# An encoder layer on one core: the last w_up stores on GpSimd's queue, and w_down's weights, late loads and weight sums placed behind left tiles

## The chip, the cores and the metric

The kernel runs on 1 core of one Trainium2 chip. The metric is the device time of one execution in microseconds (us). A core has five engines with a queue of instructions each, taken in program order: TensorE (PE, matmuls; PEld its weight loads), VectorE (DVE), ScalarE (ACT), GpSimd (POOL) and SyncE (SP). Transfers between DRAM and SBUF are issued by an engine, here nearly all by SP, and carried out by 16 DMA engines. Engines wait for each other by semaphores.

## The reference

One layer of an encoder on 2048 tokens of width 1024: two kinds of attention, gates, an output product, and then a feed-forward block. Only that block and the last norm concern this change:

```python
h2 = rms_norm(x, norm_mlp[l])
x = x + jnp.square(jax.nn.relu(h2 @ w_up[l])) @ w_down[l]
return rms_norm(x, norm_final)
```

`w_up` is 1024 x 4096 and `w_down` 4096 x 1024, everything in float32.

## The kernel before

**Products.** A float32 product is made of three matmuls (`mm3s`, L285 to L288): each operand is split into a high part, rounded by ACT (L282), and a low part, the rest, by DVE (L283); high x high is L286, high x low L287, low x high L288. On top of that, a matrix product is cut into 2 x 2 blocks and made of seven block products instead of eight, numbered 1 to 7, whose operands are blocks or sums of blocks, and whose results are added into the four output blocks.

**w_up.** For each half of the tokens (`m` = 0, 1) eight steps `q` go over the columns of w_up (`up_quad`). Each makes the seven products, and from their results, after ReLU (L1527, L1529) and square (L1530), the left tiles of w_down's seven products: blocks `uc`, sums `uchunk` and `urb`. They go to DRAM arrays `at`: `keep` (L1550) stores those of w_down's products 3 to 7. Products 1 and 2 of w_down are cut a second time into seven (`TWICE = (1, 2)`); their left tiles go to `at2[n][p]` through `keep2` (L1575). Those of p = 1, 2, 4 are the blocks themselves; for p = 5, 6, 7, 3, with m = 1, two stored blocks are read back into a tile `urb` (L1561, on POOL's queue) and added to the new ones on DVE. All stores are issued by SP, all in one order with its loads.

**w_down.** Product order is 1, 6, 2, 7, 5, 3, 4. The ordinary ones (6, 7, 5, 3, 4) take 16 steps `k`: a left tile `da` (512 KB, L1856, four buffers), its split `dah` (four buffers), a right tile (256 KB of weights `dw`, L1863, eight buffers, or a sum of such), its split `dwh` (four buffers), and 24 matmuls of 512 columns into eight PSUM banks. Product 6 also makes `t2[k]` (L1868): two differences of three `dw` blocks, kept for products 7, 5 and 4. Products 1 and 2 go through `twice` (L1900): seven sub-products in the order 1, 5, 6, 2, 7, 3, 4 of four steps each, 24 matmuls of 256 columns a step; a left tile `da` at L1924, the right tile a block, or a sum of blocks, of four weight tiles `ZW0` to `ZW3`, which `twice_right` loads (L1882, 16 loads of 256 KB). For product 2 the sums are made ahead (`twice_sums`, called in step 7 of product 6). `add_x2` (L1966) loads a piece of the residual and adds it to an output block; the adds are spread over the steps of later products (`later`). `gf`, the last norm's weights, is loaded and scaled by POOL (L2034, L2035) behind product 1.

**The order.** The code names the engine of each instruction. The position of an instruction in its engine's queue comes from a scheduler that goes by a modelled timeline and takes an instruction when its operands and buffers are expected to be ready; so a load for a later product can stand ahead of a load for an earlier one. `tc.issue_after(x)` makes what is in its block stand behind `x` in that order. The rings of w_down take the memory that w_up's rings leave, so the first instructions on them wait for w_up's last uses.

Of the kernel before, what the change touches and what calls it, by code (L numbers as in the profile page):

```python
# [92 lines left out]
def encoder_layer(ctx, tc, x, norm_mix, w_in, b_gate, sink, rpb, w_pa, w_pb, w_out,  # L93
# [52 lines left out]
    def bcast(ap1d, n):  # L146
        return bass.AP(ap1d.tensor, ap1d.offset, [[0, P], [1, n]])
# [1392 lines left out]
    def up_quad(m, q, lf, right, spread, each, rest=()):  # L1540
# [6 lines left out]

        def keep(n, a, c):
            if n not in TWICE:
                stored[0] = SY.dma_start(ats[n][2 * q + a][:, m], c).ins  # L1550
                return
            if (m, a) != (1, 0):
                keep2(n, {(0, 0): 1, (0, 1): 2, (1, 1): 4}[m, a], c)
            if m == 0:
                return
            if a == 0:
                first[n] = c
                return
            t = up_rings["rb"]()
            for i in range(2):  # L1560
                G.dma_start(t[:, i], at2[n][1 + i][q // 2][:, q % 2])  # L1561
            a11, a12, s1, s2 = (t[:, i] for i in range(4))
            add(V, s1, first[n], c)
            keep2(n, 5, s1)
            add(V, s2, s1, a11, ALU.subtract)
            keep2(n, 6, s2)
            add(V, a11, a11, first[n], ALU.subtract)
            keep2(n, 7, a11)
            add(V, a12, a12, s2, ALU.subtract)
            keep2(n, 3, a12)  # L1570
# [1 line left out]
        first = {}  # L1572

        def keep2(n, p, c):
            stored[0] = SY.dma_start(at2[n][p][q // 2][:, q % 2], c).ins  # L1575

        for n in (1, 5, 6, 2, 7, 4, 3):
            hl, (rh, rl) = lf[n], right[n]
# [274 lines left out]
    def left(n, k, part=None):  # L1853
        raw, hl = da(), dah()
        use = slice(0, 2) if part is None else slice(part, part + 1)
        SY.dma_start(raw[:, use], ats[n][k][:, use])  # L1856
        split(raw[:, use], hl[:, 0, use], hl[:, 1, use], V)
        return hl

    def w_block(k, p, j):  # L1860
        f = 4 * (k // 2) + 2 * p + k % 2
        w = dw()
        SY.dma_start(w, w_down[0][f * P : (f + 1) * P, j * BT : (j + 1) * BT])  # L1863
        return w

    t2 = [None] * 16
# [1 line left out]
    def make_t2(k):  # L1868
        b11, b12, b22 = w_block(k, 0, 0), w_block(k, 0, 1), w_block(k, 1, 1)
        t2[k] = t2_()  # L1870
        add(V, b12, b22, b12, ALU.subtract)
        add(V, t2[k], b12, b11)

    def twice_right(n):

        p, j = {1: (0, 0), 2: (1, 0)}[n]
        out = [zw() for zw in zws]
        for a in range(2):
            for qq in range(4):
                for i in range(2):  # L1880
                    f = 4 * (2 * qq + i) + 2 * p + a
                    SY.dma_start(out[qq][:, 2 * i + a], w_down[0][f * P : (f + 1) * P, j * BT : (j + 1) * BT])  # L1882
        return [r.rearrange("p (i a) (j c) -> p i a j c", a=2, j=2) for r in out]

    def wide(t):
        return t.rearrange("p (i c) -> p i c", i=2)

    def twice_sums(rs):

        out = []  # L1890
        for r in rs:
            b11, b12, b22 = r[:, :, 0, 0], r[:, :, 0, 1], r[:, :, 1, 1]
            t1, t2 = wide(p5_()), wide(p5_())
            add(V, t1, b12, b11, ALU.subtract)
            add(V, t2, b22, t1, ALU.subtract)
            add(V, b12, b22, b12, ALU.subtract)
            out.append((t1, t2))
        return out

    def twice(n, rs, sums=None):  # L1900

        b = [bank() for _ in range(4)]
        n_bank[0] += 2
        x, z, y = b[:2], b[2:], [bank() for _ in range(2)]

        def right(p, k):

            b11, b12, b21, b22 = (rs[k][:, :, a, j] for a in range(2) for j in range(2))
            t1, t2 = sums[k] if sums else (b11, b11)
            src = {1: b11, 2: b21, 3: b22, 5: t1, 6: t2, 7: b12, 4: t2}[p]  # L1910
            if p == 4:
                add(V, src, b21, t2, ALU.subtract)
            elif not sums and p in (5, 6, 7):
                add(V, src, *{5: (b12, b11), 6: (b22, b11), 7: (b22, b12)}[p], ALU.subtract)
            hl = dwh()
            hi, lo = (wide(hl[:, i]) for i in range(2))
            split(src, hi, lo, V)
            return hi, lo

        for p in ORDER_3:  # L1920
            acc = {1: x, 2: x, 5: z, 3: z, 6: y, 7: y, 4: y}[p]
            for k in range(4):
                raw, lf = da(), dah()
                SY.dma_start(raw, at2[n][p][k])  # L1924
                split(raw, lf[:, 0], lf[:, 1], V)
                hi, lo = right(p, k)
                for t in range(4):
                    ps = acc[t // 2][:, t % 2 * 256 : t % 2 * 256 + 256]
                    at = slice(t * P, (t + 1) * P)
                    for i in range(2):  # L1930
                        mm3s(ps, lf[:, 0, i, at], lf[:, 1, i, at], hi[:, i], lo[:, i],
                             p in (1, 5) and t % 2 == 0 and k == 0 and i == 0, k == 3 and i == 1)
            for i in range(2):
                ps = wide(acc[i])
                top, low = ((X2[2 * h + i][:, :, 0:256], X2[2 * h + i][:, :, 256:512]) for h in range(2))
                if p == 1:
                    A.copy(y[i], x[i])
                    continue
                out = {5: low[1], 6: top[1], 2: top[0], 7: low[1], 3: top[1], 4: low[0]}[p]
                if n == 1 and p in (5, 6, 2, 4):  # L1940
                    A.copy(out, ps)
                else:
                    add(V, out, ps, out)
# [19 lines left out]
    def add_x2(c, i, j, t):  # L1963
        r = row_of(i, t)
        xt = x2_()
        SY.dma_start(xt, x2d[r // BT][r % BT : r % BT + P, j * BT : (j + 1) * BT])  # L1966
        add(V, c, c, xt)

    sums = {}
# [54 lines left out]
            squares(Z[t], 1, 0, t)  # L2024
            finish((Z[t], W[t]), 1, t)

    ready = {1: [twice_right(1)]}
    for n in (1, 6, 2, 7, 5, 3, 4):
        if n in TWICE:
            twice(n, *ready[n])  # L2030
            if n == 2:
                later.extend((lambda t=t: early(X[t], 0, t)) for t in range(8))
            else:
                SY.dma_start(gf, bcast(norm_final, D))  # L2034
                G.tensor_scalar(gf, gf, float(D) ** 0.5, 1.0, ALU.mult, ALU.mult)  # L2035
            continue
        if n == 6 and 2 in TWICE:
            ready[2] = [twice_right(2)]
        if n == 7:
            for rows, tiles in ((Z, zws[:2]), (W, zws[2:])):  # L2040
                rows.extend(r[:, i] for zw in tiles for r in (zw(),) for i in range(4))
        for group in ((range(8),) if n != 4 else (range(4), range(4, 8))):
# [9 lines left out]
            for k in range(16):  # L2052
                if n == 6:
                    make_t2(k)
                    if k == 7 and 2 in TWICE:
                        ready[2].append(twice_sums(ready[2][0]))
                lf, rt = left(n, k, part), right_(n, k)

                if k >= end:
# [46 lines left out]
```

## Time and profile before

| what | value |
|---|---|
| median of 3 runs | 2589.79 us (2588.19 to 2592.97) |
| the profiled execution, own time | 2584.19 us |
| its span in the trace | 2582.3 us (1.9 us lie around it) |
| mean granted PE clock | 0.995 |
| ACT busy | 1353.9 us (52%) |
| DMA | 590.25 MB, mean 229 GB/s |
| last w_up matmul ends | 1957.99 us |
| product 1 of w_down starts, ends | 1964.22, 2057.41 us |

The page gives busy times by engine; the trace behind it can be asked for any stretch. Below, "PE's waits" lists what ended PE's idle times; a timeline row has start, duration, engine, line, operation, output and inputs, and in brackets the idle time before it with its releaser; "the chain of waits" is followed back from the last instruction; SPq is SP issuing a transfer, and DMA share is the mean busy share of the 16 DMA engines.

### The profile page before, as it was taken

The page shows a single profiled execution, that of the slowest core. Times are in us where ns is not written, and L with a number is a line of the kernel's source. Part 1 is how long each engine was busy: PE and PEld are TensorE (multiplying, and loading weights), DVE is VectorE, ACT ScalarE, POOL GpSimd, SP SyncE. Part 2 cuts the span into 40 slices and gives each one's busy share as a digit, 9 for nine tenths or more (in the row PEclk, how much of TensorE's full clock was granted, in tenths as well). Part 3 has the DMA queues.
Part 4 walks back from the last instruction along what each step waited for, and adds up shares of the span by engine and source line. Part 5 has one row for each costly group of instructions (what it writes and reads, how often), then busy time and mean ns, then how long its engine had stood idle before and what let it go on. Part 6 is the DMA issues. An engine that isn't in the chain of part 4 may idle for free.

```text
span 2582.3 us, 36197 instructions
## 1 busy us (share of the span) xinstructions
PE 2529.6 (98%) x12512; PEld 2137.7 (83%) x12512; DVE 1779.9 (69%) x2786; ACT 1353.9 (52%) x2421; POOL 421.8 (16%) x533
## 2 busy tenths in 40 slices
PE   8999999999999999999999999999997999999998
PEld 6788888878888888888888878888887989988887
DVE  8857676656665677656587776887777947754766
ACT  6365464557776676424255665644444534422444
POOL 1000101133446765120310000000000000000011
PEclk9999999999999999999999999999998999999999
DMA  5768868774357999688886877876659944644564
GB/s 188 222 196 255 281 216 273 245 219 122 106 148 194 242 278 258 217 305 310 300 315 208 264 257 254 300 236 218 213 198 334 370 168 157 214 158 157 184 201 162
DMA packets 365159, 590.25 MB, mean 229 GB/s; under 512 B 33912, under 2 KB 158312, under 8 KB 362928
## 3 DMA queue, kind: packets, MB, share of 16 engines
q1 hardware_dynamic: 345232, 539.03, 65.4%
q0 software_dynamic: 8800, 24.79, 3.1%
q10 hardware_dynamic: 10944, 24.12, 2.5%
q8 instruction: 99, 1.62, 0.3%
q14 instruction: 84, 0.69, 0.1%
HBM read 388.52 MB, written 199.30 MB: 228 GB/s over the span
## 4 chain that ended last, share of the span: by engine, by line
PE 83%; DMA 7%; DVE 5%; ACT 2%; issue 1%; SPq 1%; POOL 0%; DVEq 0%; POOLq 0%; ACTq 0%
PE b L288 16%; PE b L286 16%; PE b L287 16%; PE zb L286 5%; PE zb L288 5%; PE zb L287 5%; PE mm L202 3%; PE mm L204 3%; PE mm L203 3%; PE av L1141 2%; PE pt L1161 2%; PE s L1115 2%; PE pt L897 1%; DMA h2d<-ht 1%; PE av L883 1%
## 5 line engine op out<-in xcount | busy, mean ns | idle before, releaser
L286 PE MATMUL b<-dwh,dah 128*128 128x512 f32 (+1 forms) x1088 | 367.9, 347 | 11.7 <-ACT dah L282 11.7
L287 PE MATMUL b<-dwh,dah 128*128 128x512 f32 (+1 forms) x1088 | 376.3, 347 | 0.0
L288 PE MATMUL b<-dwh,dah 128*128 128x512 f32 (+1 forms) x1088 | 368.8, 347 | 2.1 <-DVE dah L283 2.1
L282 ACT CAST dah<-da 128x1024 fp32r<-128x1024 f32 (+1 forms) x152 | 145.5, 960 | 273.9 <-PE b L288 141.8
L286 PE MATMUL zb<-zh,zwhl 128*128 128x512 f32 x728 | 284.8, 392 | 3.2 <-ACT zc L493 1.4
L283 DVE TENSOR_TENSOR dah<-da,dah 128x1024 fp32r<-128x1024 f32 (+1 forms) x152 | 168.4, 1110 | 169.7 <-ACT dah L282 169.5
L287 PE MATMUL zb<-zh,zwhl 128*128 128x512 f32 x728 | 285.1, 392 | 0.0
L288 PE MATMUL zb<-zh,zwhl 128*128 128x512 f32 x728 | 283.4, 391 | 0.8 <-DVE zwhl L283 0.8
L286 PEld LDWEIGHTS b<-dwh,dah 128*128 128x128 f32 x1088 | 207.9, 191 | 37.6 <-ACT dah L282 12.8
L286 PE MATMUL b<-ubh,uwhlb 128*128 128x512 f32 x592 | 230.2, 389 | 1.2 <-DVE uc L277 1.2
L287 PE MATMUL b<-ubh,uwhlb 128*128 128x512 f32 x592 | 230.3, 389 | 0.0
L288 PE MATMUL b<-ubh,uwhlb 128*128 128x512 f32 x592 | 229.1, 389 | 0.3 <-DVE uwhlb L283 0.3
L288 PEld LDWEIGHTS b<-dwh,dah 128*128 128x128 f32 x1088 | 206.0, 191 | 28.0 <-DVE dah L283 2.8
L287 PEld LDWEIGHTS b<-dwh,dah 128*128 128x128 f32 x1088 | 207.8, 191 | 24.9
L286 PEld LDWEIGHTS zb<-zh,zwhl 128*128 128x128 f32 x728 | 136.9, 188 | 33.4 <-ACT zc L493 2.5
L288 PEld LDWEIGHTS zb<-zh,zwhl 128*128 128x128 f32 x728 | 136.9, 188 | 29.3 <-DVE zwhl L283 1.3
L287 PEld LDWEIGHTS zb<-zh,zwhl 128*128 128x128 f32 x728 | 137.0, 188 | 27.8
L202 PE MATMUL mm<-zh,whl 128*128 128x512 f32 x368 | 156.0, 424 | 2.3 <-DVE z L1019 1.2
L204 PE MATMUL mm<-zh,whl 128*128 128x512 f32 x368 | 145.8, 396 | 0.0
L203 PE MATMUL mm<-zh,whl 128*128 128x512 f32 x368 | 145.5, 395 | 0.0
L277 DVE TENSOR_TENSOR uc<-b,uc 128x512 f32<-128x512 f32 x160 | 108.4, 685 | 48.7 <-PE b L288 46.7
L286 PEld LDWEIGHTS b<-ubh,uwhlb 128*128 128x128 f32 x592 | 111.1, 188 | 24.6 <-ACT uchunk L1347 1.6
(276 smaller groups left out, 5826.4 us busy)
## 6 DMA issues: line engine op xcount, KB each, us to landing
da<-at SPq DMA_DIRECT2D x120, 512.0 KB, 4.2
at<-uc SPq DMA_DIRECT2D x172, 256.0 KB, 3.7
uraw<-in_w_up_dram SPq DMA_DIRECT2D x32, 1024.0 KB, 6.0
dw<-in_w_down_dram SPq DMA_DIRECT2D x128, 256.0 KB, 3.9
pgl<-wo_d SPq DMA_DIRECT2D x28, 1024.0 KB, 6.3
zraw<-in_w_in_dram SPq DMA_DIRECT2D x24, 1024.0 KB
z<-zg SPq DMA_DIRECT2D x64, 256.0 KB, 5.3
at<-urb SPq DMA_DIRECT2D x64, 256.0 KB, 2.2
```

What stands on the lines that cost most here:

```text
L202: PE.matmul(ps, lh, rh, start=first, stop=False)
L203: PE.matmul(ps, lh, rl, start=False, stop=False)
L204: PE.matmul(ps, ll, rh, start=False, stop=last)
L277: return eng.tensor_tensor(out=out, in0=a, in1=b, op=op).ins
L282: rounded[0] = A.copy(hi, src).ins
L283: return eng.tensor_tensor(out=lo, in0=src, in1=hi.bitcast(F32), op=ALU.subtract).ins
L286: PE.matmul(ps, lh, rh, start=first, stop=False, skip_group_check=True)
L287: PE.matmul(ps, lh, rl, start=False, stop=False, skip_group_check=True)
L288: PE.matmul(ps, ll, rh, start=False, stop=last, skip_group_check=True)
L1115: PE.matmul(ps[:, :n], q[:, i, :], kv[:, z, B_R0[i] // 4 : (B_R0[i] + B_NR[i]) // 4, 4 * B_C0[j] : 4 * (B_C0[j] + w)], start=z == 0, stop= ...
L1141: PE.matmul(po[0][:, i0 * P : (i0 + ni) * P], v[:kp, c, :], src[:kp, o : o + ni * P], start=first[0], stop=(c == 7 and z == 1), skip_group ...
L1161: last = PE.transpose(pt[:kp, at + (i - i0) * P : at + (i - i0 + 1) * P], s[i][:, rr : rr + kp], ident)
```

## The change

- Of the stores of the second token half, those of p = 5, 6, 7, 3 for products 1 and 2, and in the last step (q = 7) all, are issued by POOL instead of SP: 76 stores.
- `twice_right` no longer issues its 16 loads at once. It returns a generator that issues two at a time: for product 1 one pair ahead of each left tile, for product 2 one pair in each step of product 6 from step 2 on.
- Each `dw` load stands behind the load of the third last left tile, each `x2` load and `gf` behind the last one; the first difference of `t2` and of each set of sums stands behind the last left tile's low part on DVE.
- The four sets of sums for product 2 are made one at a time in steps 8, 10, 12 and 14 of product 6.
- `gf` is loaded ahead of product 7 and scaled by ACT.

```diff
--- before.py
+++ after.py
@@ -1547,7 +1547,8 @@
 
         def keep(n, a, c):
             if n not in TWICE:
-                stored[0] = SY.dma_start(ats[n][2 * q + a][:, m], c).ins
+                queue = G if m and q == 7 else SY
+                stored[0] = queue.dma_start(ats[n][2 * q + a][:, m], c).ins
                 return
             if (m, a) != (1, 0):
                 keep2(n, {(0, 0): 1, (0, 1): 2, (1, 1): 4}[m, a], c)
@@ -1572,7 +1573,8 @@
         first = {}
 
         def keep2(n, p, c):
-            stored[0] = SY.dma_start(at2[n][p][q // 2][:, q % 2], c).ins
+            queue = G if m and (q == 7 or p in (5, 6, 7, 3)) else SY
+            stored[0] = queue.dma_start(at2[n][p][q // 2][:, q % 2], c).ins
 
         for n in (1, 5, 6, 2, 7, 4, 3):
             hl, (rh, rl) = lf[n], right[n]
@@ -1853,14 +1855,17 @@
     def left(n, k, part=None):
         raw, hl = da(), dah()
         use = slice(0, 2) if part is None else slice(part, part + 1)
-        SY.dma_start(raw[:, use], ats[n][k][:, use])
-        split(raw[:, use], hl[:, 0, use], hl[:, 1, use], V)
+        das.append(SY.dma_start(raw[:, use], ats[n][k][:, use]).ins)
+        last_lo[0] = split(raw[:, use], hl[:, 0, use], hl[:, 1, use], V)
         return hl
+
+    last_lo, das = [None], []
 
     def w_block(k, p, j):
         f = 4 * (k // 2) + 2 * p + k % 2
         w = dw()
-        SY.dma_start(w, w_down[0][f * P : (f + 1) * P, j * BT : (j + 1) * BT])
+        with tc.issue_after(das[-3]):
+            SY.dma_start(w, w_down[0][f * P : (f + 1) * P, j * BT : (j + 1) * BT])
         return w
 
     t2 = [None] * 16
@@ -1868,36 +1873,40 @@
     def make_t2(k):
         b11, b12, b22 = w_block(k, 0, 0), w_block(k, 0, 1), w_block(k, 1, 1)
         t2[k] = t2_()
-        add(V, b12, b22, b12, ALU.subtract)
+        with tc.issue_after(last_lo[0]):
+            add(V, b12, b22, b12, ALU.subtract)
         add(V, t2[k], b12, b11)
 
     def twice_right(n):
 
         p, j = {1: (0, 0), 2: (1, 0)}[n]
         out = [zw() for zw in zws]
-        for a in range(2):
-            for qq in range(4):
-                for i in range(2):
-                    f = 4 * (2 * qq + i) + 2 * p + a
-                    SY.dma_start(out[qq][:, 2 * i + a], w_down[0][f * P : (f + 1) * P, j * BT : (j + 1) * BT])
-        return [r.rearrange("p (i a) (j c) -> p i a j c", a=2, j=2) for r in out]
+
+        def load():
+            for a in range(2):
+                for qq in range(4):
+                    for i in range(2):
+                        f = 4 * (2 * qq + i) + 2 * p + a
+                        SY.dma_start(out[qq][:, 2 * i + a], w_down[0][f * P : (f + 1) * P, j * BT : (j + 1) * BT])
+                    yield
+
+        return [r.rearrange("p (i a) (j c) -> p i a j c", a=2, j=2) for r in out], load()
 
     def wide(t):
         return t.rearrange("p (i c) -> p i c", i=2)
 
     def twice_sums(rs):
 
-        out = []
         for r in rs:
             b11, b12, b22 = r[:, :, 0, 0], r[:, :, 0, 1], r[:, :, 1, 1]
             t1, t2 = wide(p5_()), wide(p5_())
-            add(V, t1, b12, b11, ALU.subtract)
+            with tc.issue_after(last_lo[0]):
+                add(V, t1, b12, b11, ALU.subtract)
             add(V, t2, b22, t1, ALU.subtract)
             add(V, b12, b22, b12, ALU.subtract)
-            out.append((t1, t2))
-        return out
-
-    def twice(n, rs, sums=None):
+            yield t1, t2
+
+    def twice(n, rs, loads, sums=None):
 
         b = [bank() for _ in range(4)]
         n_bank[0] += 2
@@ -1920,9 +1929,10 @@
         for p in ORDER_3:
             acc = {1: x, 2: x, 5: z, 3: z, 6: y, 7: y, 4: y}[p]
             for k in range(4):
+                next(loads, None)
                 raw, lf = da(), dah()
-                SY.dma_start(raw, at2[n][p][k])
-                split(raw, lf[:, 0], lf[:, 1], V)
+                das.append(SY.dma_start(raw, at2[n][p][k]).ins)
+                last_lo[0] = split(raw, lf[:, 0], lf[:, 1], V)
                 hi, lo = right(p, k)
                 for t in range(4):
                     ps = acc[t // 2][:, t % 2 * 256 : t % 2 * 256 + 256]
@@ -1963,7 +1973,8 @@
     def add_x2(c, i, j, t):
         r = row_of(i, t)
         xt = x2_()
-        SY.dma_start(xt, x2d[r // BT][r % BT : r % BT + P, j * BT : (j + 1) * BT])
+        with tc.issue_after(das[-1]):
+            SY.dma_start(xt, x2d[r // BT][r % BT : r % BT + P, j * BT : (j + 1) * BT])
         add(V, c, c, xt)
 
     sums = {}
@@ -2024,19 +2035,19 @@
             squares(Z[t], 1, 0, t)
             finish((Z[t], W[t]), 1, t)
 
-    ready = {1: [twice_right(1)]}
+    ready = {1: list(twice_right(1))}
     for n in (1, 6, 2, 7, 5, 3, 4):
         if n in TWICE:
             twice(n, *ready[n])
             if n == 2:
                 later.extend((lambda t=t: early(X[t], 0, t)) for t in range(8))
-            else:
-                SY.dma_start(gf, bcast(norm_final, D))
-                G.tensor_scalar(gf, gf, float(D) ** 0.5, 1.0, ALU.mult, ALU.mult)
             continue
         if n == 6 and 2 in TWICE:
-            ready[2] = [twice_right(2)]
+            ready[2] = list(twice_right(2))
         if n == 7:
+            with tc.issue_after(das[-1]):
+                SY.dma_start(gf, bcast(norm_final, D))
+            A.activation(gf, gf, AF.Copy, scale=float(D) ** 0.5)
             for rows, tiles in ((Z, zws[:2]), (W, zws[2:])):
                 rows.extend(r[:, i] for zw in tiles for r in (zw(),) for i in range(4))
         for group in ((range(8),) if n != 4 else (range(4), range(4, 8))):
@@ -2052,8 +2063,13 @@
             for k in range(16):
                 if n == 6:
                     make_t2(k)
-                    if k == 7 and 2 in TWICE:
-                        ready[2].append(twice_sums(ready[2][0]))
+                    if k >= 2 and 2 in TWICE:
+                        next(ready[2][1], None)
+                    if k == 6 and 2 in TWICE:
+                        sums2 = twice_sums(ready[2][0])
+                        ready[2].append([])
+                    if k >= 8 and k % 2 == 0 and 2 in TWICE:
+                        ready[2][2].append(next(sums2))
                 lf, rt = left(n, k, part), right_(n, k)
 
                 if k >= end:
```

How the rows move where w_up gives way to w_down, first on **SP**. Before, the tail of the `ZW` loads and the first left tiles (`da`, sub-product 1, `at1_1_k`):

```order
L1882 DMA ZW2_2024_18319<-in_w_down_dram 128x512 x2
L1882 DMA ZW0_2022_18317<-in_w_down_dram 128x512 x2
L1550 DMA at4_15_11490<-uc_2003_18141 128x512
L1882 DMA ZW1_2023_18318<-in_w_down_dram 128x512 x2
L1882 DMA ZW2_2024_18319<-in_w_down_dram 128x512 x2
L1924 DMA da_2026_18343<-at1_1_0_11539 128x1024
L1924 DMA da_2029_18375<-at1_1_1_11540 128x1024
L1924 DMA da_2032_18407<-at1_1_2_11541 128x1024
L1924 DMA da_2035_18439<-at1_1_3_11542 128x1024
L1863 DMA dw_2114_19299<-in_w_down_dram 128x512
L1550 DMA at5_14_11505<-uchunk_2006_18205 128x512
L1863 DMA dw_2115_19301<-in_w_down_dram 128x512
```

and further on, where the first left tile of sub-product 5 (`at1_5_0`) stands:

```order
L1966 DMA x2_2355_21140<-x2d0_148 128x512
L1575 DMA at2_6_3_11578<-urb_2004_18178 128x512
L1966 DMA x2_2361_21179<-x2d2_150 128x512
L1924 DMA da_2038_18473<-at1_5_0_11543 128x1024
L1966 DMA x2_2367_21218<-x2d2_150 128x512
L1966 DMA x2_2373_21257<-x2d2_150 128x512
L1550 DMA at5_15_11506<-uchunk_2008_18230 128x512
L1575 DMA at2_7_3_11586<-urb_2004_18178 128x512
L1575 DMA at2_3_3_11590<-urb_2004_18178 128x512
L1966 DMA x2_2379_21296<-x2d2_150 128x512
L1924 DMA da_2041_18506<-at1_5_1_11544 128x1024
```

Now, from the first `ZW` load on:

```order
L1890 DMA ZW3_2025_18320<-in_w_down_dram 128x512 x4
L1890 DMA ZW0_2022_18317<-in_w_down_dram 128x512 x2
L1934 DMA da_2026_18329<-at1_1_0_11539 128x1024
L1890 DMA ZW1_2023_18318<-in_w_down_dram 128x512 x2
L1934 DMA da_2029_18363<-at1_1_1_11540 128x1024
L1890 DMA ZW2_2024_18319<-in_w_down_dram 128x512 x2
L1934 DMA da_2032_18397<-at1_1_2_11541 128x1024
L1934 DMA da_2035_18431<-at1_1_3_11542 128x1024
L1890 DMA ZW0_2022_18317<-in_w_down_dram 128x512 x2
L1890 DMA ZW1_2023_18318<-in_w_down_dram 128x512 x2
L1890 DMA ZW2_2024_18319<-in_w_down_dram 128x512 x2
L1934 DMA da_2038_18467<-at1_5_0_11543 128x1024
```

The left tiles stand between the pairs of `ZW`; the stores are gone from here, and `dw`, `x2` and `gf` no longer stand ahead of sub-product 5.

On **DVE**, around the low part of the first left tile (`dah_2027`), before:

```order
L277 TENSOR_TENSOR ZW1_2023_18318<-ZW1_2023_18318 128x2x256
L277 TENSOR_TENSOR uc_2005_18204<-uc_1995_17996,uchunk_2006_18205 128x512
L277 TENSOR_TENSOR ZW3_2025_18320<-ZW3_2025_18320 128x2x256
L277 TENSOR_TENSOR ZW2_2024_18319<-ZW2_2024_18319 128x2x256
L277 TENSOR_TENSOR urb_2004_18178<-urb_2004_18178 128x512
L283 TENSOR_TENSOR dah_2027_18344<-da_2026_18343,dah_2027_18344 128x1024
L277 TENSOR_TENSOR ZW3_2025_18320<-ZW3_2025_18320 128x2x256
L277 TENSOR_TENSOR uchunk_2008_18230<-uc_1998_18067,uc_2003_18141 128x512
L277 TENSOR_TENSOR urb_2004_18178<-urb_2004_18178,uc_1995_17996 128x512
```

and now, where `dwh_2028` is the low part of the first right tile:

```order
L277 TENSOR_TENSOR urb_2001_18100<-urb_2001_18100 128x512
L277 TENSOR_TENSOR uc_2003_18141<-b_152_18054,uc_1996_18011 128x512
L283 TENSOR_TENSOR dwh_2028_18334<-ZW0_2022_18317,dwh_2028_18334 128x512
L277 TENSOR_TENSOR uc_2003_18141<-b_150_18026,uc_2003_18141 128x512
L277 TENSOR_TENSOR ZW0_2022_18317<-ZW0_2022_18317 128x2x256
L277 TENSOR_TENSOR uc_1995_17996<-b_151_18039,uc_1995_17996 128x512
L283 TENSOR_TENSOR dah_2027_18330<-da_2026_18329,dah_2027_18330 128x1024
L277 TENSOR_TENSOR uc_1997_18052<-b_149_18013,uc_1997_18052 128x512
L283 TENSOR_TENSOR dwh_2031_18368<-ZW1_2023_18318,dwh_2031_18368 128x512
```

It stands four rows behind the first right tile's low part, ahead of w_up's last sums `uchunk`, `uc_2005` and `urb_2004`, which it stood among before.

On **POOL**, the last rows of w_up before:

```order
L1561 DMA urb_2001_18100<-at1_1_3_11542 128x512
L1561 DMA urb_2001_18100<-at1_2_3_11554 128x512
L1561 DMA urb_2004_18178<-at2_1_3_11570 128x512
L1561 DMA urb_2004_18178<-at2_2_3_11582 128x512
L2035 TENSOR_SCALAR gf_2009_18271<-gf_2009_18271 128x1024
```

and now, from behind the pair of loads of `urb_2001` on:

```order
L1577 DMA at1_4_3_11566<-uc_2000_18096 128x512
L1577 DMA at1_5_3_11546<-urb_2001_18100 128x512
L1577 DMA at1_6_3_11550<-urb_2001_18100 128x512
L1577 DMA at1_7_3_11558<-urb_2001_18100 128x512
L1577 DMA at1_3_3_11562<-urb_2001_18100 128x512
L1551 DMA at4_14_11489<-uc_2002_18123 128x512
L1551 DMA at4_15_11490<-uc_2003_18141 128x512
L1551 DMA at5_14_11505<-uchunk_2006_18205 128x512
L1577 DMA at2_4_3_11594<-uc_1996_18011 128x512
L1551 DMA at7_14_11537<-uc_1997_18052 128x512
L1551 DMA at6_14_11521<-uchunk_2006_18205 128x512
L1562 DMA urb_2004_18178<-at2_1_3_11570 128x512
```

Eleven stores stand between the last two pairs of `urb` loads, and the scaling of `gf` is gone.

## The prediction

> **What bounds the kernel now.** I read the page's busy shares first. TensorE (PE) is busy nearly the whole span, so time can only come out of the places where it stands or runs slowly.
>
> ```profile
> PE 2529.6 (98%) x12512; PEld 2137.7 (83%) x12512; DVE 1779.9 (69%) x2786; ACT 1353.9 (52%) x2421; POOL 421.8 (16%) x533
> ```
>
> Next come PE's waits from 1940 us to the end, the part of the span in which the w_down products run:
>
> ```profile
> PE b L286 <- ACT dah L282: 11.7, 4, 6.2
> PE b L288 <- DVE dah L283: 2.1, 3, 1.1
> ```
>
> These two rows are all of that view: 13.8 us, every one a wait for `dah`, a left tile split into its high part (ACT) and low part (DVE). PE's timeline says where (the bracket is the idle time ahead and who ended it):
>
> ```profile
> 1957.60 0.39 PE L288 MATMUL b<-ubh,uwhla 128*128 128x512 f32 x1
> ...
> 1964.22 0.58 PE L286 MATMUL b<-dwh,dah 128*128 128x256 f32 x1 [6.23 <-ACT dah L282]
> ...
> 1984.32 0.39 PE L286 MATMUL b<-dwh,dah 128*128 128x256 f32 x1 [4.46 <-ACT dah L282]
> ...
> 2057.84 0.50 PE L286 MATMUL b<-dwh,dah 128*128 128x512 f32 x1 [0.43 <-ACT dah L282]
> ```
>
> The last w_up matmul ends at 1957.60 + 0.39 = 1957.99. The first w_down product, `twice(1)`, gets its first left tile 6.23 us later, stops again 4.46 us when its second sub-product (p=5) begins, and gives way to product 6 at 2057.84. Idle time is not the whole loss, as windows of 2 us show (span, PE busy, granted clock, DMA share, GB/s):
>
> ```profile
> 1966.00:1968.00 2.00, 1.45 (x7) 0.50 1.04 402
> ...
> 1972.00:1974.00 2.00, 2.00 (x19) 1.00 1.03 385
> 1984.00:1986.00 2.00, 1.25 (x6) 0.70 1.07 404
> 1986.00:1988.00 2.00, 2.00 (x11) 0.50 1.03 414
> ```
>
> After each of the two long gaps the granted clock falls to 0.50, and the same 2 us hold 11 matmuls where they hold 19 at 1.00. The Trainium skill, "TensorE: Matmul & The Clock Gate", Part 1, has the clock halved after an idle window of about 3.4 us; the 6.23 and 4.46 us gaps here agree, and by it a gap shorter than that would cost its own length and no more.
>
> The pace at full clock is in the chain of waits:
>
> ```profile
> 1992.60 0.24 PE b L288 x2
> 1995.48 0.24 PE b L288 x2
> ...
> 2053.08 0.24 PE b L288 x2
> ```
>
> One step (one left tile with one right tile, 24 matmuls) takes 1995.48 − 1992.60 = 2.88 us, and from 1992.60 to 2053.08 there are 21 such steps without a loss. `twice` has 7 x 4 = 28 steps: 80.64 us. Started at 1957.99 it would end at 2038.63; product 6 starts at 2057.84. So **19.2 us** are lost here: 13.8 idle and 5.4 through the slow clock. This is the ceiling for any change to this boundary.
>
> Why the tiles are late, from the chain and from SP's queue:
>
> ```profile
> 1948.36 5.16 DMA at<-urb
> 1953.54 5.13 DMA ZW<-in_w_down_dram
> ...
> 1981.95 6.88 DMA da<-at
> ```
>
> ```profile
> 1929.89 1.76 SPq L1882 DMA_DIRECT2D ZW<-in_w_down_dram  x4
> 1943.95 0.33 SPq L1575 DMA_DIRECT2D at<-uc  x1
> ...
> 1955.43 2.32 SPq L1924 DMA_DIRECT2D da<-at  x4
> ...
> 1981.95 1.65 SPq L1924 DMA_DIRECT2D da<-at  x2
> ```
>
> SP issues in program order. Between 1931.7 and 1943.95 it stands before a store whose data is not computed; the weights and the first four left tiles lie behind it, the tiles leaving at 1955.43. The next tiles (p=5) come behind eight `dw`, `gf`, eight `x2` and late stores, and the chain's `da` leaves at 1981.95 and lands 6.88 us later.
>
> **The change, part by part.** *First left tiles.* By SP's new order the first tile leaves behind six `ZW` loads, about 1933. The second waits for memory of the last w_up split, which is this row:
>
> ```profile
> 1942.80 1.23 DVE L283 TENSOR_TENSOR uwhla<-uraw,uwhla 128x1024 fp32r<-128x1024 f32 x1 [4.21 <-ACT uwhla L282]
> ```
>
> So SP still stands until 1944.0, but now only one tile and no store is behind the point that mattered, and the first `dah` is split when DVE comes to it. DVE reaches it about 1950.6 by today's times of the rows ahead (the w_up eviction before it needs a PE bank that is full at 1957.99 − 3 x 2.72 = 1949.8, if PE's last four groups of 12 matmuls, 2.72 us each by the 0.227 us a matmul of the chain further down, end in order) and has it at 1951.7, before 1957.99. The 6.23 and 1.10 us go, and with them the slow clock: I take the first gap at zero.
>
> *Tiles of p=5.* From 1944 SP issues, ahead of the first of them, four left tiles less one, eight `ZW`: 1.5 + 2.0 = 3.5 MB, and it itself is 0.5; the stores beside are up to 11 x 0.25 = 2.75 MB, about 1.8 of them by then. 5.8 MB at the rates of these windows
>
> ```profile
> 1960.00:1970.00 10.00, 4.68 (x20) 4.39 (x21) 10.00 (x16) 5.24 (x6) 0.00 (x0) 0.55 1.03 406
> 1970.00:1980.00 10.00, 9.86 (x78) 9.65 (x77) 9.87 (x14) 2.54 (x5) 4.36 (x1) 0.94 1.06 375
> 2062.00:2149.00 87.00, 87.00 (x402) 72.72 (x401) 43.41 (x54) 27.98 (x35) 0.00 (x0) 1.00 0.45 160
> ```
>
> (after PE, PEld, DVE, ACT and POOL: clock, DMA share, GB/s), some 390, are 15 us: it lands about 1960, PE wants it at 1957.99 + 4 x 2.88 = 1969.5. The transfer is no longer late; the second rows show who is: DVE is busy 10.00 and 9.87 of 10 us. Its work is not reduced, only reordered: 29 instructions stand between the first `dah` and the low part of p=5's first, 4 of them wide. Their pace:
>
> ```profile
> 1959.26 0.68 DVE L277 TENSOR_TENSOR ZW<-ZW 128x512 f32<-128x512 f32 x1
> 1959.87 0.68 DVE L283 TENSOR_TENSOR dwh<-ZW,dwh 128x512 fp32r<-128x512 f32 x1
> ...
> 1965.28 1.22 DVE L283 TENSOR_TENSOR dah<-da,dah 128x1024 fp32r<-128x1024 f32 x1
> 1966.41 0.68 DVE L277 TENSOR_TENSOR ZW<-ZW 128x512 f32<-128x512 f32 x1
> ```
>
> 0.60 us narrow and 1.14 wide, start to start: 25 x 0.60 + 4 x 1.14 = 19.6, and 0.8 of waiting for a w_up bank: done at 1951.7 + 20.4 = 1972.1. The third matmul of that step wants it at 1969.5 + 0.24. So a **new wait of 2.4 us** takes the place of 4.46; the next two steps have 3 narrow and 1 wide each, 2.94 against 2.88, another 0.1, and then DVE gets ahead. Bounds: none, if DVE starts its part 2.4 us sooner, and, if the first low part ends only at 1954.3 (three narrow and one wide behind today's first `dwh`, at 1951.3), 5.0 us, which by the row of 4.46 above brings the slow clock back at about 3 us. I take 2.5: the counts are exact and the starting point is the nearest row.
>
> *Inside product 6.* The moved differences (`t2`, sums for product 2) and 24 MB of loads (16 x 0.5 left, 48 x 0.25 `dw`, 16 x 0.25 `ZW`) fall here. One step takes
>
> ```profile
> 2061.78 1.81 PE b L288 x8
> 2067.22 1.81 PE b L288 x8
> ```
>
> 5.44 us (24 matmuls of 512 columns), the product 87 us: 24 / 87 = 276 GB/s, under the 406 seen above. DVE: per step one wide and three narrow, 2.94 x 16 = 47, and 12 for the sums, 7.2: 54 of 87. Both fit; cost nothing, hidden under PE. The start keeps its 0.43 us, for the same copy of a bank stands before the cast. *`gf` on ACT:* one pass near
>
> ```profile
> L282 ACT CAST dah<-da 128x1024 fp32r<-128x1024 f32 (+1 forms) x152 | 145.5, 960 | 273.9 <-PE b L288 141.8
> ```
>
> 0.96 us on an engine busy 28 of 87: nothing; without that cover 1 us. *Stores on POOL.* POOL's issue is
>
> ```profile
> 1954.23 1.09 POOL L1561 DMA_DIRECT2D urb<-at  x2 [23.93 <-DMA ZW<-in_w_down_dram]
> ```
>
> 0.55 us each against 0.33 on SP: 76 x 0.55 = 42 us in all, on an engine busy 421.8 us of the span. Behind its waiting stores stands only the next load of `urb`; the last now leaves about 1960 instead of 1954.23, and DVE wants it at about 1975. The Trainium skill, "DMA: Bandwidth & Descriptors", section "Issuing engines are not separate DMA queues", says that all issuers share the same 16 engines and only issue time is saved; by it this move is worth 76 x 0.33 us of issue, off the path. The share of 1.03 agrees with shared engines, but the row of 1943.95 shows order, not bandwidth, holding SP.
>
> *Sum:* 19.2 − 2.6 − 0.4 = **16.2 us** less: 2584.19 − 16.2 = 2568.0 for the profiled execution. That one lies 5.6 us under the median of the runs, 2589.79; the loss is in both, so against the median 2573.6.
>
> **Rivals.** (1) *DVE late.* The new wait is 5.0 us and the clock halves for about 3 more: 19.2 − 8.5 = about 11 us gained, 2579. For it: DVE is full. (2) *No wait at all*: 19.2, 2570.6. For it: nothing but the bound. (3) *The transfers stay late.* If the tiles are still held by bytes that go first, the two gaps stay, 2590, whatever the order. Against it: some 4.5 MB (`dw`, `gf`, `x2`) no longer leave ahead of p=5. (4) *Slower: tied loads late in product 6.* Each `dw` now leaves only behind the third last left tile, and DVE, which runs in order, stands at the difference until it lands, with the next `dah` behind it. Landing takes (issues in 1900 to 2100 us)
>
> ```profile
> dw<-in_w_down_dram SPq DMA_DIRECT2D x58, 256.0 KB, 5.4
> ...
> x<-x2d SPq DMA_DIRECT2D x8, 256.0 KB, 6.1
> ```
>
> 5.4 us; the eight `dw` buffers at three a step give 2.67 x 5.44 = 14.5 us. It decides if landing and issue pass that: 16 steps times 1.0 us eat the gain, and 1.35 us a step make it 2595. The same holds for `x2` (6.1) in the later products, where SP can run ahead by the four buffers of `da`, 4 x 5.44 = 21.8 us.
>
> **Chances.** Forecast (2571.5 to 2576) 0.58; (1) 0.20; (2) 0.07; (3) 0.08; (4) 0.07. A measurement of this kernel tells about 0.2%, 5.2 us. Faster by more than that: 0.58 + 0.20 + 0.07 = 0.85; same 0.08; slower 0.07. The range leaves out (3) and (4), 0.15: from 2569, under (2) by the scatter of the runs (1.6 below the median), to 2582, rival (1) and the scatter above (3.2).
>
> **What would show it.** Right: no row of over 3.4 us in PE's waits after 1957, clock 1.00 throughout, a wait of 2 to 3 us on DVE's `dah` at about 1969, product 6 starting near 2041.5, and SP's first `da` before 1935. Wrong: a wait for ACT `dah` behind a `da` transfer at 1958 or 1969 (3); several waits on `dwh` or `dah` spaced by 5.44 us after 2042 (4); a clock of 0.50 near 1972 (1).

## The result and the profile after

The changed kernel took 2570.27 us (median of 4 runs, 2568.25 to 2572.95) beside 2588.99 us of the kernel before (4 runs): ratio 0.9928, 95% interval 0.9910 to 0.9947, 18.7 us less. Run twice more beside the experiments it took 2574.48 (6 runs, ratio 0.9953, 0.9935 to 0.9970) and 2571.52 (6 runs, ratio 0.9937, 0.9916 to 0.9959).

Executions of one kernel differ by up to 14.5 us (2566.62 to 2581.10 in the first of these sets of six), and the profiles say where most of it arises: ahead of w_up, and so ahead of the change. In three profiles of the changed kernel the first w_up matmul starts at 1347.37, 1354.78 and 1344.29 us and the last ends at 1961.15, 1970.56 and 1958.07, while what follows repeats to 1.4 us. So the experiments go by two stretches: the **boundary**, from the end of the last w_up matmul to the first matmul of product 6 (80.64 us if PE never stood or slowed, by the 28 steps of 2.88 us), and the **rest**, from there to the end.

| | before | changed |
|---|---|---|
| profiled execution | 2584.19 us | 2571.70 us |
| w_up ends | 1957.99 us | 1961.15 us |
| boundary | 99.85 us | 84.68 us |
| rest | 524.46 us | 524.07 us |

The change is worth 15.2 us at the boundary and 0.4 behind it. The profiled execution shows only 12.5 because its w_up ended 3.2 us late. The change also moves stores inside w_up, but an effect there does not show: w_up takes 612.8 us before and 613.8, 615.8 and 613.8 in the changed kernel, and 612.0 to 616.6 over all the kernels below.

PE's waits of the changed kernel from 1930 us to the end, one row where there were two:

```profile
PE b L288 <- DVE dah L283: 2.5, 1, 2.5
```

Its PE timeline (start, duration, line, output and inputs, in brackets the idle time and its releaser):

```profile
1960.76 0.39 PE L288 MATMUL b<-ubh,uwhla 128*128 128x512 f32 x1
1960.98 0.28 PE L286 MATMUL b<-dwh,dah 128*128 128x256 f32 x1
...
1975.59 0.39 PE L288 MATMUL b<-dwh,dah 128*128 128x256 f32 x1 [2.46 <-DVE dah L283]
...
2045.83 0.40 PE L286 MATMUL b<-dwh,dah 128*128 128x512 f32 x1
```

`twice(1)` starts on the heels of w_up, the wait of 6.23 us is gone, the one of 4.46 at p=5 has become 2.46, and product 6 starts with no wait. SP's queue:

```profile
1935.81 0.53 SPq L1934 DMA_DIRECT2D da<-at  x1
1936.43 0.88 SPq L1890 DMA_DIRECT2D ZW<-in_w_down_dram  x2
1947.20 0.33 SPq L1934 DMA_DIRECT2D da<-at  x1
...
1956.82 2.70 SPq L1934 DMA_DIRECT2D da<-at  x2
```

The first left tile leaves ahead of SP's stand of 9.9 us (1937.3 to 1947.2, for memory of w_up), and the tiles of p=5 leave from 1956.82 on, where they left from 1977.42 on. DVE, which has no idle time from 1955.74 up to these rows:

```profile
1973.72 0.68 DVE L277 TENSOR_TENSOR uchunk<-uchunk,uc 128x512 f32<-128x512 f32 x1
1974.32 1.22 DVE L283 TENSOR_TENSOR dah<-da,dah 128x1024 fp32r<-128x1024 f32 x1
```

The low part that PE waits for comes straight behind a sum of w_up: DVE's queue, not a transfer, is what is late.

### The profile page after: what moved, and what is told of

Same layout as the page of the kernel before. It is cut to its first block, busy times and chain, and to the rows that moved or that the text cites. A ratio compares the mean times of both kernels' runs of the same rounds, so it can differ in the third digit from the quotient of the medians.

```text
span 2569.9 us, 36087 instructions
## 1 busy us (share of the span) xinstructions
PE 2525.9 (98%) x12512; PEld 2133.6 (83%) x12512; DVE 1780.9 (69%) x2786; ACT 1355.1 (53%) x2422; POOL 458.3 (18%) x608
## 4 chain that ended last, share of the span: by engine, by line
PE 86%; DMA 5%; DVE 4%; ACT 2%; issue 1%; SPq 0%; POOL 0%; ACTq 0%; POOLq 0%; DVEq 0%
PE b L288 17%; PE b L286 17%; PE b L287 17%; PE zb L288 5%; PE zb L286 5%; PE zb L287 5%; PE mm L202 3%; PE mm L203 3%; PE mm L204 3%; PE av L1141 2%; PE pt L897 1%; PE pt L1161 1%; PE s L1115 1%; PE b L202 1%; PE b L204 1%
```

## The experiments

All boundary and rest times are from profiles, one for each kernel. The changed kernel's three profiles give boundaries of 84.68, 84.67 and 83.29 us, so a difference of 1.4 us between two kernels is not an effect by itself; then the waits and the order of the queues have to show it. Differences of some hundredths in the rest are rounding of the span.

| kernel | boundary, us | PE's waits over 0.4 us there | rest, us |
|---|---|---|---|
| before | 99.85 | 6.23, 1.10, 4.46, 0.43, 0.61, 0.52, 0.43 | 524.46 |
| e1, stores only | 99.38 | 0.62, 3.54, 7.63, 0.43, 0.98 | 526.02 |
| e11, load ties only | 90.43 | 6.21, 1.32 | 525.20 |
| e12, stores and load ties | 87.85 | 0.62, 3.54 | 524.06 |
| changed | 84.68 | 2.46 | 524.07 |
| e2, changed, stores on SP | 88.80 | 0.52, 0.48, 5.23 | 524.42 |
| e3, changed, loads untied | 93.31 | 2.46, 5.88 | 524.13 |
| e4, changed, sums untied | 84.60 | 2.46 | 524.12 |
| e5, changed, weights at once | 86.65 | 0.62, 3.54 | 524.13 |
| e6, changed, w_up sums on GpSimd | 91.60 | 1.56, 6.62, 0.46 | 524.09 |
| e8, changed, closer tie | 84.66 | 2.46 | 524.09 |
| e10, changed, sums behind tiles | 81.78 | 0.41 | 524.12 |

**e1: the stores alone.**

```diff
-                stored[0] = SY.dma_start(ats[n][2 * q + a][:, m], c).ins
+                queue = G if m and q == 7 else SY
+                stored[0] = queue.dma_start(ats[n][2 * q + a][:, m], c).ins
...
-            stored[0] = SY.dma_start(at2[n][p][q // 2][:, q % 2], c).ins
+            queue = G if m and (q == 7 or p in (5, 6, 7, 3)) else SY
+            stored[0] = queue.dma_start(at2[n][p][q // 2][:, q % 2], c).ins
```

> Only the 76 stores are issued by GpSimd; loads and sums as before. Measure: time from the end of the last w_up matmul to the start of product 6 (before 99.85 us, changed kernel 84.68, 80.64 without a loss). Theory A (the order on SP made the tiles late): the held store and the late stores are gone from SP, so the first left tiles leave before or right behind 1944 and the 6.23 us gap goes; but 8 dw, gf and 8 x2 still stand ahead of the first tile of p=5, about 9 MB from 1946 at 390 GB/s, so it lands near 1970 and a gap of 2 to 6 us with half clock stays: 86 to 92 us. Theory B (the 16 DMA engines are full, who issues is the same): nothing changes, 97 to 100 us. Theory C (the stores are all of it): 84 to 86 us.

99.38 us, 0.5 less: above theory A's 86 to 92, and by the number theory B's 97 to 100. But B has nothing change, and the waits did. Its PE timeline and SP's queue:

```profile
1960.52 0.39 PE L286 MATMUL b<-dwh,dah 128*128 128x256 f32 x1 [0.62 <-ACT dah L282]
1964.80 0.58 PE L288 MATMUL b<-dwh,dah 128*128 128x256 f32 x1 [3.54 <-DVE dah L283]
...
1985.89 0.58 PE L286 MATMUL b<-dwh,dah 128*128 128x256 f32 x1 [7.63 <-ACT dah L282]
...
2066.57 0.50 PE L286 MATMUL b<-dwh,dah 128*128 128x512 f32 x1 [1.65 <-ACT dah L282]
```

```profile
1943.10 4.15 SPq L1926 DMA_DIRECT2D da<-at  x4
1957.21 2.98 SPq L1865 DMA_DIRECT2D dw<-in_w_down_dram  x6
...
1963.49 11.97 SPq L1968 DMA_DIRECT2D x<-x2d  x8
1976.53 3.18 SPq L1926 DMA_DIRECT2D da<-at  x4
```

The first tiles leave 16.8 us ahead of w_up's end (1959.90), where before they left 2.6 us ahead of it, and the first gap shrinks from 6.23 + 1.10 to 0.62 + 3.54 (e5 shows what is left there). But the tiles of p=5 still leave at 1976.53, behind `dw`, `gf` and `x2`: PE gets to p=5 sooner and waits 7.63 there instead of 4.46. What one gap gave the other took back. The last row is a new wait inside product 6, for which e1's rest is 1.6 us longer than before: over both stretches the stores alone gained nothing.

**e11 and e12: the ties of the loads, without and with the stores.** On the kernel before, and on e1 (`das` lists the loads of the left tiles, as in the change):

```diff
-        SY.dma_start(w, w_down[0][f * P : (f + 1) * P, j * BT : (j + 1) * BT])
+        with tc.issue_after(das[-3]):
+            SY.dma_start(w, w_down[0][f * P : (f + 1) * P, j * BT : (j + 1) * BT])
...
-        SY.dma_start(xt, x2d[r // BT][r % BT : r % BT + P, j * BT : (j + 1) * BT])
+        with tc.issue_after(das[-1]):
+            SY.dma_start(xt, x2d[r // BT][r % BT : r % BT + P, j * BT : (j + 1) * BT])
...
-                SY.dma_start(gf, bcast(norm_final, D))
+                with tc.issue_after(das[-1]):
+                    SY.dma_start(gf, bcast(norm_final, D))
```

> The kernel before with the ties of dw, x2 and gf behind left tiles alone; stores on SP, product 1's weights at once, sums as before. The first tiles still stand behind the held store and 16 weight loads: the first gap of some 6 us stays. Those of p=5 stand behind late stores instead of 17 loads. If the ties act by themselves: the second gap falls to 1 to 4 us, 90 to 95 us from the end of w_up to product 6. If the ties act only together with the move of the stores: as before, 97 to 100 us.

> The kernel before with these ties and with the stores moved to GpSimd: no pairs of weights between left tiles, no ties or steps of sums, gf on GpSimd. Theory: SP's order around the boundary is then that of e5_block, 86 to 87.5 us, with the gap of about 3.5 us in p=1 and none at p=5. If the remaining edits (sums, gf) carry something: 88 us or more, or waits behind the start of product 6 (stretch to the end over 524.5 us).

e11: 90.43, as the first reading had it; the second gap, expected at 1 to 4 us, is gone. PE's timeline of e11 has the old first gap and nothing at p=5:

```profile
1966.67 0.58 PE L286 MATMUL b<-dwh,dah 128*128 128x256 f32 x1 [6.21 <-ACT dah L282]
1969.22 0.58 PE L288 MATMUL b<-dwh,dah 128*128 128x256 f32 x1 [1.32 <-DVE dah L283]
```

The 1.1 us that e11's rest is longer than the changed kernel's lie behind its last matmul.

e12: 87.85, 0.35 over the expected 86 to 87.5, with the two waits of e5 to the hundredth; it is 1.2 us longer than e5 because more of the slow clock follows (7.2 − 4.16 = 3.0 us beyond the waits, 1.9 in e5), so no effect of the remaining edits shows there. Its rest is that of the changed kernel, so scaling `gf` on ACT and making the sums by steps, which e12 lacks, are worth nothing behind the boundary either. The four cases together: stores −0.5 by themselves (not an effect), ties −9.4, both −12.0. Once the ties are in, the stores are worth 2.6; the waits alone fall by 3.4.

**e2: the changed kernel with the stores on SP.**

```diff
-                queue = G if m and q == 7 else SY
+                queue = SY
...
-            queue = G if m and (q == 7 or p in (5, 6, 7, 3)) else SY
+            queue = SY
```

> The loads and sums as in the changed kernel, but all stores issued by SP as before. Theory A: the first left tile stands behind two stores of urb and leaves about 1946, in time; those of p=5 and p=6 stand behind stores that wait for DVE's last w_up sums (to about 1979 in the changed kernel), so small waits of some us come at p=5 and p=6: 85 to 92 us. Theory that the loads' order is all of it: 84 to 85.5 us. Theory B (bytes alone): as the changed kernel too, 84 to 85.5 us, for the bytes ahead are the same.

88.80, in theory A's range and not in that of the two others; the wait came at p=5 alone, not at p=6. Its PE timeline, SP's queue, and ACT and DVE at the second tile of p=5:

```profile
1978.98 0.58 PE L288 MATMUL b<-dwh,dah 128*128 128x256 f32 x1 [5.23 <-DVE dah L283]
```

```profile
1963.47 0.33 SPq L1551 DMA_DIRECT2D at<-uc  x1
1964.15 0.74 SPq L1551 DMA_DIRECT2D at<-uchunk  x1
1965.44 0.32 SPq L1577 DMA_DIRECT2D at<-uc  x1
1966.11 0.32 SPq L1934 DMA_DIRECT2D da<-at  x1
```

```profile
1971.77 1.05 ACT L282 CAST dah<-da 128x1024 fp32r<-128x1024 f32 x1 [0.97 <-DMA da<-at]
1977.70 1.22 DVE L283 TENSOR_TENSOR dah<-da,dah 128x1024 fp32r<-128x1024 f32 x1
```

The second tile of p=5 leaves behind stores of w_up's last sums and has landed when ACT takes it at 1971.77, but DVE comes to it 5.9 us later, without idle time ahead of it. The stores are worth 4.1 us here, with the same bytes. So the stores act by order, not by bytes; how much of it is the tile's place on SP, and how much the place that the scheduler then gives it on DVE, was not separated.

**e3: the ties of the loads undone.** Taken from the `dw`, `x2` and `gf` loads, of which the first stands for all:

```diff
-        with tc.issue_after(das[-3]):
+        if True:
             SY.dma_start(w, w_down[0][f * P : (f + 1) * P, j * BT : (j + 1) * BT])
```

> The changed kernel without the ties of dw, x2 and gf to left tiles. The order then puts them ahead of the third tile of p=5. Theory A: that tile leaves behind some 17 loads, 12 MB from 1944 at 390 GB/s, and lands about 1975, with its split behind DVE's queue: a second gap of 1 to 5 us in p=5 beside the 2.5 us, 86 to 91 us. If the ties are worth nothing: 84.7 us.

93.31, 8.6 more, beyond theory A's 91: the new gap is 5.88 where 1 to 5 was expected, and more slow clock follows. The new gap, and the tile behind it, from PE's timeline and SP's queue:

```profile
1987.31 0.58 PE L286 MATMUL b<-dwh,dah 128*128 128x256 f32 x1 [5.88 <-ACT dah L282]
```

```profile
1972.18 5.33 SPq L1977 DMA_DIRECT2D x<-x2d  x6
1978.89 0.32 SPq L1934 DMA_DIRECT2D da<-at  x1
```

It is the third tile of p=5, which stands behind six `x2` loads and leaves at 1978.89.

**e5: product 1's weights at once again.**

```diff
+        if n == 1:
+            for _ in loads:
+                pass
         for p in ORDER_3:
```

> The changed kernel, but the 16 weight loads of product 1 are issued at once again, ahead of the first left tile. Theory A: nothing to lose here, for SP is held until about 1944 by w_up's memory either way and the four first tiles still leave by 1946 to 1950: 84.5 to 86 us. Rival (the interleaving is what closes the first gap): the first tile lands behind 4 MB of weights, about 1956 to 1960, and the first gap comes back with 2 to 5 us and half clock: 88 to 93 us.

86.65, 2.0 more, between the two. The rival's gap comes back (0.62 and 3.54 in p=1), but not for its reason. SP's queue, the fourth left tile in the chain of waits, and the first tile's low part on DVE:

```profile
1947.36 51.47 SPq L1937 DMA_DIRECT2D da<-at  x17
```

```profile
1950.93 8.27 DMA da<-at
```

```profile
1967.64 1.22 DVE L283 TENSOR_TENSOR dah<-da,dah 128x1024 fp32r<-128x1024 f32 x1
```

The first left tile leaves behind all 16 weights, 16.7 us ahead of w_up's end (1964.02) instead of 25.3. Even the fourth has landed at 1959.20, 4.8 us ahead of that end. What is late is the low part: DVE has no idle time in the 15 us ahead of it, and makes eight sums of weights there where the changed kernel made one. The scheduler goes by when it expects the loads, so the new order on SP changed DVE's order too. e1 and e12 have the same two waits and the same place of this low part, 4.8 us behind w_up's end. By p=5 DVE is through its queue, so the wait of 2.46 there is gone: one wait takes the place of the other.

**e4 and e8: the parts said to matter later.** e4 takes `issue_after` from the sums, in `make_t2` and in the same way in `twice_sums`; e8 moves one index:

```diff
-        with tc.issue_after(last_lo[0]):
+        if True:
             add(V, b12, b22, b12, ALU.subtract)
```

```diff
-        with tc.issue_after(das[-3]):
+        with tc.issue_after(das[-1]):
             SY.dma_start(w, w_down[0][f * P : (f + 1) * P, j * BT : (j + 1) * BT])
```

> The changed kernel without the ties of the weight sums (t2 and the sums for product 2) to left tiles. Theory A: nothing changes up to the start of product 6, since the dw loads stay behind the left tiles and so the sums cannot come early: 84.7 us from the end of w_up to product 6, and no wait of PE behind it. Rival (the ties keep DVE from standing at sums whose loads are late): waits of some us at left tiles inside product 6, spaced by its steps of 5.44 us, and the stretch from product 6 to the end grows by 2 to 10 us over 524.1.

> The changed kernel with each dw load tied behind the last left tile's load instead of the third last. Theory (rival 4 of the prediction does not bite: eight dw buffers and four da buffers leave a lead of some 14 us over a landing of 5.4): no wait of PE in product 6 and later, 524 us from the start of product 6 to the end. If the tie is what sets the lead: the lead falls by two steps of 5.44 us, and waits of 1 us or more come in each step of product 6, 16 us or more in all.

84.60 and 84.66, rest 524.12 and 524.09, and no wait of PE behind the one at p=5. The ties of the sums do nothing here, and the lead of the `dw` loads is long enough for the closer tie, with which the first of them leaves 64.6 us behind w_up's end instead of 58.8.

**e6: w_up's last sums on GpSimd.** DVE's queue is what is left, so the last eight sums of w_up go to the other engine that can add:

```diff
-                    add(V, s1, a21, a22)
+                    E = G if m and q == 7 else V
+                    add(E, s1, a21, a22)
```

and so for the three sums behind it.

> The changed kernel with the eight last sums of w_up's last step (both halves a) computed by GpSimd instead of DVE. Five narrow instructions, 3.0 us, go from DVE's queue between the first left tile and that of p=5. If DVE's full queue is what is left (theory), the wait of 2.46 us goes and with it the slow clock behind it: 80.6 to 81.3 us, some 3.5 to 4 us less than the changed kernel. Rival (GpSimd's sums are slow and the last loads of urb stand behind three of them, so DVE waits for urb ahead of the tiles of p=5): a new wait at p=5's later tiles, 83 to 90 us. A copy of gf took GpSimd 4.36 us for 128x1024, so one of these sums should take 2 to 4 us.

91.60, 6.9 more than the changed kernel; 2580.25 us in 12 runs, ratio to before 0.9969 (0.9957 to 0.9981). The rival's number, but not its reason. GpSimd's sums are quick, on its timeline:

```profile
1959.90 1.32 POOL L277 TENSOR_TENSOR uc<-uc,uc 128x512 f32<-128x512 f32 x1
1961.19 1.74 POOL L277 TENSOR_TENSOR uchunk<-uchunk,uc 128x512 f32<-128x512 f32 x1
...
1965.61 1.38 POOL L277 TENSOR_TENSOR uc<-uc,uchunk 128x512 f32<-128x512 f32 x1
1966.96 1.29 POOL L277 TENSOR_TENSOR uchunk<-uc,uc 128x512 f32<-128x512 f32 x1
```

DVE's of the same times are not:

```profile
1959.99 3.49 DVE L277 TENSOR_TENSOR ZW<-ZW 128x512 f32<-128x512 f32 x2
...
1965.78 3.02 DVE L277 TENSOR_TENSOR ZW<-ZW 128x512 f32<-128x512 f32 x1
...
1970.46 0.68 DVE L277 TENSOR_TENSOR ZW<-ZW 128x512 f32<-128x512 f32 x1
```

A sum of 0.68 us takes 3.02 while GpSimd adds, and ends half a us behind GpSimd's. From 1957.68 to the low part at 1979.31 DVE has no idle time, so it does not wait for `urb`, as the rival had it: its 17 narrow and 2 wide rows there take 21.6 us, where their pace of 0.60 and 1.14 gives 12.5. The Trainium skill, "SBUF — State Buffer", section "Who interferes with whom", says that a DVE instruction with two SBUF inputs contends with a GpSimd instruction that reads SBUF; these rows agree.

**e10: the sums of later sub-products behind the left tiles.** `los` lists the low parts of the left tiles in order:

```diff
             if p == 4:
-                add(V, src, b21, t2, ALU.subtract)
+                with tc.issue_after(los[-5]):
+                    add(V, src, b21, t2, ALU.subtract)
             elif not sums and p in (5, 6, 7):
-                add(V, src, *{5: (b12, b11), 6: (b22, b11), 7: (b22, b12)}[p], ALU.subtract)
+                with tc.issue_after(los[-5]):
+                    add(V, src, *{5: (b12, b11), 6: (b22, b11), 7: (b22, b12)}[p], ALU.subtract)
```

> The changed kernel with each weight sum of product 1's later sub-products (p = 5, 6, 7 and 4, on DVE) tied behind the left tile's low part four steps earlier, so that the sums for p=6, 7 and 4 no longer stand ahead of the first left tile of p=5. Six narrow sums go from ahead of it (3.6 us; two of p=5's come nearer, in a place where DVE waits for a bank anyway). If only DVE's order holds PE there: its low part is done 2.5 to 3 us earlier, the wait of 2.46 us falls to at most 0.4 at p=5's later tiles, and no half clock follows: 80.6 to 81.3 us from the end of w_up to product 6, 3.4 to 4 us less than the changed kernel. Rival (the work is only pushed on and DVE, full up to 1990, makes the wait later): one wait of 2 to 3 us at the last tile of p=5 or the first of p=6, 83 to 85 us.

PE's waits from 1940 us to the end:

```profile
PE b L288 <- DVE dah L283: 0.4, 1, 0.4
```

81.78, 0.5 over the expected range: the wait and the slow clock are gone, and the push-on of the rival did not come. The runs give 2570.11 us (6 runs, ratio 0.9928, 0.9906 to 0.9950) beside 2571.52 of the changed kernel: by the time alone the two are not told apart; by the boundary e10 is 1.5 to 2.9 us shorter.

**The changed kernel again.**

> The changed kernel once more, beside e6_pool_sums on the same chip. 84 to 85.5 us from the end of w_up to product 6, a wait of about 2.5 us on DVE at the first tile of p=5 and half clock for about 3 us behind it; 15 to 20 us under the kernel before.

> The changed kernel beside e10_sums_behind on the same chip: 84 to 85 us from the end of w_up to product 6, as in its two profiles before; the total 13 to 19 us under the kernel before, by the scatter of the stages ahead of w_up's end.

84.67 us beside e6 and 83.29 beside e10, the second under its expected 84 to 85, both with the wait of 2.46; 13.4 and 18.7 us under the kernel before by the runs. What differs is in the last section.

## Why the prediction was right, and where it was off

- **The loss of 19.2 us and its two gaps.** Right. e11 has the first gap alone, and e12 and e5 have none at p=5; the boundary falls accordingly, and the rest stays.
- **First gap to zero.** Right. The first tile's low part was forecast 6.3 us ahead of w_up's end (1951.7 beside 1957.99) and came 6.2 ahead of it, in this row of DVE's timeline of the changed kernel:

```profile
1953.72 1.21 DVE L283 TENSOR_TENSOR dah<-da,dah 128x1024 fp32r<-128x1024 f32 x1
```

  Both parts of that working were needed: the early tiles, and DVE's new order, by which it comes to the first of them in time. e1, e5 and e12 have the early tiles without that order, and keep waits of 0.62 and 3.54 us.

- **A new wait of 2.4 us on DVE at the first tile of p=5.** Right in place, engine and size: 2.46, and by its working: from the first low part's end to that of p=5 the count gave 20.4 us, and 20.6 were measured (1954.93 to 1975.54). e10 shows it was DVE's order: with the same work behind that tile instead of ahead of it, it goes.
- **"I take 2.5", and no slow clock behind it.** This term was mis-sized. I let the clock fall only in rival (1), at 5.0 us, and expected 1.00 throughout. It fell behind 2.46 us in five profiles of six, and cost about 1.4 us (84.67 beside 83.29). The Trainium skill, "TensorE: Matmul & The Clock Gate", Part 1, has the clock halved after an idle window of about 3.4 us and so would have let this gap pass; here the measurement decides.
- **0.43 us kept at product 6.** Off: there was no wait there.
- **Loads and sums of product 6 hidden.** Right: PE is full, DVE 57 of 87 us (forecast 54), 241 GB/s (forecast 276) in this window of the changed kernel:

```profile
2046.00:2133.00 87.00, 87.00 (x385) 72.01 (x385) 57.33 (x78) 26.77 (x34) 0.00 (x0) 1.00 0.68 241
```

  e8 shortened the lead on which rival (4) turns, and PE still did not wait.
- **Stores on POOL.** The forecast was that their own cost is hidden and that order, not bandwidth, held SP. e1, e11, e12 and e2 show that order is right but that the held store was only one of two blocks: no gain alone, 2.6 us with the ties, 4.1 in the whole change.
- **The sum.** Forecast 16.2; the stretches give 15.6 (15.2 and 0.4), the first comparison of runs 18.7 and the later ones 13.4 and 18.7, with intervals that hold both 16.2 and 15.6. By its number the first, 2570.27, lies under the 2571.5 to 2576 of the forecast and on the 2570.6 of rival (2), which has no wait at all. The trace shows the forecast's wait, not rival (2). The 3 us between 18.7 and 15.6 are not in the boundary or the rest; the profiles have scatter of that size ahead of them, and nothing shows these 3 us to be the change's. That this comparison came out so high is then luck.

## What to carry to other kernels

Where PE waits twice in a row, removing the first wait's cause alone can give nothing: the second tile leaves when it left before, and PE only waits for it longer. So follow each late tile to its place in the issuing queue, and clear all that stands ahead of them together. Where a scheduler sets the order, look at the other engines' queues again, for a new order of loads moves their instructions too. When the transfers are then early, count the instructions of the busiest engine ahead of each tile: that count gave the wait that was left to within 0.1 us, and moving work on that engine behind the tile removed it, while moving work to GpSimd made it longer.

## What the runs showed of the hardware

*A wait of 2.46 us can halve PE's clock, or not.* The same wait, from the same instruction, in windows of 2 us (span, PE busy, clock, DMA share, GB/s), first the changed kernel's profile:

```profile
1972.00:1974.00 2.00, 1.14 (x10) 1.00 1.00 408
1974.00:1976.00 2.00, 0.41 (x3) 0.98 0.47 180
1976.00:1978.00 2.00, 2.00 (x11) 0.50 0.89 297
```

and its profile taken beside e10:

```profile
1970.00:1972.00 2.00, 0.05 (x1) 1.00 0.60 240
1972.00:1974.00 2.00, 1.49 (x12) 1.00 0.85 277
1974.00:1976.00 2.00, 2.00 (x18) 1.00 0.66 260
```

The clock fell in the profiles of the changed kernel, e3, e4, e8 and its first repeat, and not in the second. The waits of 1.56 us in e6 and 1.65 in e1, and those under 1 us at full clock, brought no fall; every wait of 3.54 us or more did. What decides at 2.46 us was not tested.

*DVE and GpSimd at once.* In e6 a DVE sum of 0.68 us took up to 3.02 beside GpSimd sums of 1.3 to 2.2 us, so that two engines together did less than one: from 1965.61 to 1968.80 they made three sums, where DVE alone, at one each 0.60 us, makes five. The kernel before has a weaker case: beside the scaling of `gf` on GpSimd (4.36 us from 1974.29) five DVE instructions kept their 0.68 us, and only the sixth, which ends half a us behind GpSimd's, was slow, in this row of DVE's timeline before:

```profile
1977.67 1.50 DVE L283 TENSOR_TENSOR dwh<-ZW,dwh 128x512 fp32r<-128x512 f32 x1
```
